# A hybrid transformer step on one core: second part reordered, sixteen z blocks, some elementwise work on GpSimd

## The chip, the cores and the metric

One of the eight cores of a Trainium2 chip runs the whole program in one launch. The metric is the device time of one execution in microseconds (us), a median over executions. The core has a matmul engine (TensorE, PE in the profile; its weight loads are PEld), a vector engine (VectorE, DVE), a scalar engine (ScalarE, ACT), a general one (GpSimd, POOL) and a queue engine that issues most transfers (SyncE, SP).

## The reference

One layer over 512 prompt tokens and 8 x 4 sample tokens, width 2048, everything in float32. In short:

```
xn = rmsnorm(x, g_mix);  proj = xn @ w_in      # q k v iq ik iw xb yb qm
A  = top-k sparse attention (indexer relu scores -> top-k -> softmax over those keys)
B  = RG-LRU(conv4(xb)) * gelu(yb)              # block-diagonal gates, linear recurrence
C  = memory cross-attention(qm, mk, mv)        # 4 heads, 256 memory tokens
x  = x + (sum_n sigmoid(xn @ w_gate[n]) * (branch_n @ w_br[n])) @ w_o
# product-key experts: 16384 experts, 8 heads, 128 x 128 keys, top-16
s  = q(xn2) . sub_keys;  top16 of each half;  top16 of the sums -> expert ids e, weights g
x  = x + sum_k g_k * gelu(u[e_k] . xn2) * v[e_k]
y  = rmsnorm(x, g_final)
```

The outputs are y, the keys and values, the indexer keys, the last convolution inputs, the recurrence's last state and the memory keys and values.

## The kernel before, in words

The 544 tokens are columns and are worked on in two parts: the first (288 columns: 32 sample and 256 prompt tokens, `xF`) and the second (256 prompt columns, `xA`). Every weight goes through one path, a **unit** of 128x1024 numbers (512 KB): `stream` (L233) loads it into a buffer `raw` (L241, SyncE's queue), ScalarE rounds it to `hi` (L221), VectorE makes the rest `lo = raw - hi` (L222), and TensorE does 24 matmuls, for each of 8 chunks hi by x-high, hi by x-low, lo by x-high (L271, L1400). `raw`, `hi` and `lo` are rings of three buffers each (RAW, HL); `widen` adds buffers to the rings for a stage.

The stages in order: memory keys; `branches(0)`, `merge(0)`, `output_proj(0)` for the first part; the first part's expert queries (`pairs(route1, ...)`); `branches(1)`, `merge(1)`, `output_proj(1)` for the second part; the second part's queries, mixed with the first fifty expert rows `up(j)`, and the gate matrices; then sixteen groups, each with the remaining `up(j)`, eight blocks `gated(j)` and `down(g)` (16 units of `v`, then `acc += ...` on VectorE, L1403). `gated(j)` loads a block `gl` (or takes the fresh `ge`), multiplies it by the gate `gt` on VectorE (L1385) and splits it into `zh` (ScalarE) and `zl` (VectorE), rings of nine.

`branches(1)` goes over 45 channels of 128 columns, two units each: first the 8 memory queries (with the memory heads as background work), then the indexer (1 + 8), the 8 queries, keys, values, and last the 16 channels of the recurrence. Attention heads (`attn_head`) and the recurrence (`lru`) start when the selection of the keys is done, beside the last 16 channels; the memory heads' and the indexer's tiles share a pool (`memo`) that closes first.

The side work is written as generators in queues (`Background`): `pump` is called once per chunk (three matmuls), each queue then has rate/8 of a step. bg and bg2 carry heads, selection, attention and recurrence, bg3 the gather: 224 experts' rows of u and 224 of v (1 MB each, fetched by GpSimd's indirect transfers, L1142, and worked on by VectorE with a 128x2048 instruction each, L1190 and L1198) for the first 224 columns. Each row's transfer and its VectorE instruction are tied to the matmul issued last before them (`pace`). Columns 224 and up go through the dense path.

What a scheduler makes of it: instructions are listed per engine by priority (those under `urgent()` first) as far as the scheduler's own model holds them ready; on the chip each engine takes its list strictly in order, and so does SyncE's queue.

Of the kernel before, what the change touches and what calls it, by code (L numbers as in the profile page):

```python
# [35 lines left out]
P0 = NS  # L36
# [5 lines left out]
GL = 4  # L42
AHEAD_UP = 50
# [132 lines left out]
def program(tc, ins, outs):  # L176
# [33 lines left out]
    bg, bg2, bg3 = Background(), Background(), Background()  # L210
    tracks = (bg, bg2, bg3)
# [178 lines left out]
    def branches(part):  # L390
# [5 lines left out]
        prompt = slice(P0 + qbs[0] * 128, P0 + qbs[0] * 128 + HB)  # L396
        pp = None if first else ps_p
        br = ExitStack()
        stg = pool("stage", br)
        ap = pool("ap", br)  # L400
# [61 lines left out]
        mp = pool("mp", memo)  # L462
        if first:
            qms = mp.tile([128, 8, NS], F, name="qms")
            mos = mp.tile([64, 512], F, name="mos")
# [73 lines left out]
        left = bg.queue[-1] if bg.queue else None  # L539
        bg.rate = 1.1 if first else 2.0  # L540
        for h in range(4):
            if h == 3 and not first:
                bg.drain(left)
                route1.weights()
                start_gather()
                rps.close()
                bg3.rate = 0.5
                bg.rate = 1.0
            qm = []
            for i in range(2):  # L550
                s = staged(CH_QM + 2 * h + i)
                if first:
                    nc.vector.tensor_copy(qms[:, 2 * h + i], s[:, :P0])
                qm.append(s)
            bg.add(mem_head(h, qm))
        if first:
            bg.add(mem_sample())


        xp_ = pool("ix", memo)  # L560
# [127 lines left out]
        memo.close()  # L688
# [3 lines left out]
        lp = pool("lr", lrs)  # L692
# [89 lines left out]
        bp = pool("bc", lrs)  # L782

        def attn_head(h):
            n = h // 4
            s = bp.tile([128, HB], F, name="qh", bufs=2)
            nc.sync.dma_start(s, outs["proj"][CH_Q + h, :, prompt])
# [88 lines left out]
        bg.drain()  # L876
        if first:
            nc.sync.dma_start(o_dram[0:8, :, :P0].rearrange("h p s -> p h s"), osm)
        else:
            nc.sync.dma_start(outs["hout"].rearrange("c p n -> p c n"), hl)  # L880
        lrs.close()
# [46 lines left out]
    def output_proj(c0, mo, xg, o0, rs):  # L928
# [5 lines left out]
        for d in range(ND):  # L934
# [8 lines left out]
            add_square(ssum, x2, wp.tile([128, n_], F, name="sq"), d == 0, nc.gpsimd)  # L943
# [13 lines left out]
    rps = ExitStack()  # L957
    rp = pool("rp", rps, side="right")
# [13 lines left out]
    rq = pool("rq", rts)  # L972
    def token_rms(t, c0, rows):
# [35 lines left out]
    class Route:  # L1009
# [14 lines left out]
        def tmp(self, name, dt=F, bufs=2):  # L1024
            return rp.tile([128, 3, 16], dt, name=name, bufs=bufs)[:, :self.nt]

        def lists(self, h, i, qT):

            c = 2 * h + i
            SI = rp.tile([128, 2, 3, 16], F, name=f"si{i}", bufs=LAG)[:, :, :self.nt]  # L1030
# [11 lines left out]
            sc = rp.tile([128, 384], F, name="sc", bufs=3)  # L1042
# [13 lines left out]
        def head(self, h, lists):  # L1056
            nt, ts = self.nt, slice(self.t0, self.t0 + self.nt)
            c2 = rp.tile([128, 2, 3, ncand], F, name="cand", bufs=2)[:, :, :nt]
# [25 lines left out]
        def weights(self):  # L1084
# [5 lines left out]
            sm = rp.tile([128, 24], F, name="gsum")[:, :8 * nt]  # L1090
# [4 lines left out]
    tiles1 = [(0, 128), (128, 128), (256, 32)]  # L1095
    tiles2 = [(0, 128), (128, 128)]
    for t, (c0, rows) in enumerate(tiles1):
        token_rms(t, c0, rows)

    def query(c, xg):  # L1100
        p = project(ins["w_pq"][c], [xg], ND, ps_p)
        qT = rp.tile([128, HA], F, name="qT", bufs=2)[:, :p.shape[-1]]
        with urgent():
            nc.scalar.copy(qT, p)
        return qT

    route1, route2 = Route(0, tiles1), Route(3, tiles2)
    bg2.add(norm())
    bg2.rate = 0.6
    bg.rate = 0.6  # L1110

# [15 lines left out]
    share["pool"] = 0  # L1127
# [345 lines left out]
```

## Time and profile before

| | us |
|---|---|
| median of 3 runs | 4518.69 (4518.44 to 4528.5) |
| profiled execution | 4522.26 |
| its span, first to last instruction | 4520.5 |
| PE busy, share of the span | 4168.4 (92%) |
| DVE busy | 3443.5 (76%) |
| ACT busy | 1930.1 (43%) |
| POOL busy | 1268.6 (28%) |
| mean granted clock of TensorE | 0.961 of full |

A matmul counts as busy for longer than it holds up the next one, so a stretch is read by how many matmuls it issued, not by the busy share. A clock of 1.00 is the upper of TensorE's two levels (2.4 GHz), 0.50 the lower (1.2 GHz). VectorE's average of 76% is made of stages between 48% and 90%.

### The profile page before, as it was taken

The numbers are of one execution on the slowest core, as the hardware profiler recorded it, in microseconds if no ns is written. First come the engines' busy times: TensorE is split into PE (matmuls) and PEld (weight loads), VectorE is DVE, ScalarE is ACT, GpSimd is POOL, SyncE is SP. The second block draws the span as 40 slices with busy tenths as digits, with TensorE's granted clock in tenths as the row PEclk, the third lists the DMA queues.
The fourth block names the chain that finished last, engine by engine and source line by source line (L and its number), as shares of the span: only waits on it lengthen the run. The fifth ranks groups of instructions, "written<-read, shape, count | busy, mean of one in ns | idle before, by whom it ended". The sixth has DMA issues, their size and how long they took to land. (4 is left out here: it accounts for less than half of the span.)

```text
span 4520.5 us, 75499 instructions
## 1 busy us (share of the span) xinstructions
PE 4168.4 (92%) x29283; PEld 3998.3 (88%) x29283; DVE 3443.5 (76%) x5192; ACT 1930.1 (43%) x2940; POOL 1268.6 (28%) x1159
## 2 busy tenths in 40 slices
PE   8999899999986977799889889979999999999998
PEld 7868699999985765799889879979899999999998
DVE  6447444455796875688887899878887999997997
ACT  5334653344432436544443359623333333333333
POOL 3021410001233111345442333312222333322333
PEclk9999999999998987899999999999999999999999
DMA  8656555556546764799987669999988999998995
GB/s 259 216 200 218 162 158 173 166 172 192 174 147 204 271 241 147 254 368 366 364 318 247 225 231 352 371 344 352 341 304 308 371 371 372 368 373 263 380 374 181
DMA packets 381256, 1231.75 MB, mean 272 GB/s; under 512 B 51296, under 2 KB 166752, under 8 KB 319968
## 3 DMA queue, kind: packets, MB, share of 16 engines
q1 hardware_dynamic: 312288, 746.64, 48.6%
q0 software_dynamic: 68608, 480.28, 27.8%
q8 instruction: 230, 3.77, 0.3%
q14 instruction: 130, 1.06, 0.1%
HBM read 1166.46 MB, written 60.22 MB: 271 GB/s over the span
## 5 line engine op out<-in xcount | busy, mean ns | idle before, releaser
L221 ACT CAST hi<-raw 128x1024 fp32r<-128x1024 f32 x1140 | 1191.6, 1049 | 1640.5 <-PE mm L271 821.6
L222 DVE TENSOR_TENSOR lo<-raw,hi 128x1024 fp32r<-128x1024 f32 x1140 | 1424.0, 1253 | 440.2 <-ACT hi L221 430.2
L271 PE MATMUL mm<-xgd,hi 128*128 128x320 f32 (+1 forms) x4608 | 1011.7, 309 | 4.0 <-ACT hi L221 4.0
L271 PEld LDWEIGHTS mm<-xgd,hi 128*128 128x128 f32 x4608 | 766.1, 189 | 4.3 <-ACT hi L221 4.2
L271 PE MATMUL mm<-xgd,lo 128*128 128x320 f32 (+1 forms) x2304 | 711.6, 309 | 21.1 <-DVE lo L222 21.0
L1400 PE MATMUL mm<-zh,hi 128*128 128x320 f32 x2048 | 638.8, 313 | 44.4 <-ACT zh L221 40.2
L1400 PE MATMUL mm<-zh,lo 128*128 128x320 f32 x2048 | 638.2, 313 | 9.8 <-DVE lo L222 9.6
L1142 POOL DMA_INDIRECT row<-in_un,idx x224 | 380.7, 1699 | 927.6 <-PE mm L271 388.9
L1400 PE MATMUL mm<-zl,hi 128*128 128x320 f32 x2048 | 638.1, 312 | 1.6 <-DVE zl L222 1.6
L271 PE MATMUL mm<-xF,hi 128*128 128x288 f32 x2976 | 624.2, 303 | 2.1 <-ACT stage L424 1.4
L1142 POOL DMA_INDIRECT row<-in_vn,idx x224 | 406.0, 1813 | 756.3 <-PE mm L1400 242.3
L271 PE MATMUL mm<-xA,hi 128*128 128x256 f32 x2976 | 550.7, 287 | 27.9 <-ACT hi L221 18.4
L1198 DVE SCALAR_TENSOR_TENSOR gacc<-row,hv,gacc 128x2048 f32<-128x2048 f32 x221 | 521.8, 2361 | 52.5 <-DMA row<-in_vn,idx 30.7
L1190 DVE SCALAR_TENSOR_TENSOR row<-row,xnat 128x2048 f32<-128x2048 f32 x224 | 513.3, 2292 | 55.6 <-DMA row<-in_un,idx 18.4
L271 PEld LDWEIGHTS mm<-xA,hi 128*128 128x128 f32 x2976 | 467.7, 193 | 42.2 <-ACT hi L221 20.3
L271 PEld LDWEIGHTS mm<-xF,hi 128*128 128x128 f32 x2976 | 483.7, 189 | 23.1 <-issue 17.6
L271 PEld LDWEIGHTS mm<-xgd,lo 128*128 128x128 f32 x2304 | 435.6, 189 | 27.3 <-DVE lo L222 27.0
L271 PE MATMUL mm<-xF,lo 128*128 128x288 f32 x1488 | 445.7, 300 | 0.0
L271 PE MATMUL mm<-xA,lo 128*128 128x256 f32 x1488 | 426.7, 287 | 10.4 <-DVE lo L222 10.3
L1400 PEld LDWEIGHTS mm<-zh,hi 128*128 128x128 f32 x2048 | 390.3, 191 | 48.4 <-ACT zh L221 42.5
L1400 PEld LDWEIGHTS mm<-zh,lo 128*128 128x128 f32 x2048 | 390.2, 191 | 12.5 <-DVE lo L222 12.3
L1400 PEld LDWEIGHTS mm<-zl,hi 128*128 128x128 f32 x2048 | 390.1, 191 | 3.3 <-DVE zl L222 2.9
(370 smaller groups left out, 6317.8 us busy)
## 6 DMA issues: line engine op xcount, KB each, us to landing
raw<-in_u SPq DMA_DIRECT2D x256, 512.0 KB, 7.1
raw<-in_v SPq DMA_DIRECT2D x256, 512.0 KB, 7.0
raw<-in_w_gate SPq DMA_DIRECT2D x192, 512.0 KB, 4.9
raw<-in_w_in SPq DMA_DIRECT2D x180, 512.0 KB, 4.4
raw<-in_w_br SPq DMA_DIRECT2D x96, 512.0 KB, 3.7
raw<-in_w_pq SPq DMA_DIRECT2D x64, 512.0 KB, 4.4
raw<-in_w_o SPq DMA_DIRECT2D x64, 512.0 KB, 4.6
g_dram<-gs SPq DMA_DIRECT2D x10, 2048.0 KB, 7.6
```

Of the source, the lines that this page charges most:

```text
L221: nc.scalar.copy(hi, src)
L222: eng.tensor_tensor(lo, src, hi.bitcast(F), op=OP.subtract)
L271: last["mm"] = nc.tensor.matmul(p[:, i, :n], a[:, s], chunk(b[which], u + k), start=(u + k == 0 and pr == 0), stop=(u + k == k_chunks - 1 ...
L1142: i = nc.gpsimd.indirect_dma_start(out=r, out_offset=None, in_=ins[table], in_offset=bass.IndirectOffsetOnAxis(ap=ind[:, s:s + 1], axis=0))
L1190: j = nc.vector.scalar_tensor_tensor(r, r, 1.0, xn, op0=OP.mult, op1=OP.mult, accum_out=h)
L1198: j = nc.vector.scalar_tensor_tensor(acc, r, h, acc, op0=OP.mult, op1=OP.add)
L1400: last["mm"] = nc.tensor.matmul(p[:, 0, :NTA], a[:, s], b, start=(k == 0 and pr == 0), stop=(k == 7 and pr == 2))
```

## The change

Seven things change.

1. `branches(1)`: the memory queries and heads move behind keys and values, before the recurrence's channels. The first 8 channels are now the indexer's. `start_gather` moves from behind six memory channels to behind the fourth indexer channel. The recurrence gets a queue of its own (bg4), the heads' next query is loaded one head ahead (`load_q`), and the rates change (attention 1.1 instead of 1.6).
2. The first part's third token tile (32 columns of a 288-column part) is taken out of `route1`: its query columns are kept in `qk`, and `odd_lists` makes its lists and heads beside the second part's indexer.
3. While `share["pool"]` is 4 (first part's queries, all of `branches(1)`, second part's queries up to three `up` behind them) the low part of every fourth unit is made by GpSimd instead of VectorE: 8 of 32 units, 23 of 90, and 18 of the queries and rows behind.
4. `gated`: the product of block and gate goes to GpSimd, 128 times.
5. The rings `zh` and `zl` grow from nine to sixteen; for that `widen(zs0, 2, 0)` goes, so in the last stage the ring `raw` has three buffers instead of five.
6. The last four additions of squares in `output_proj` go from GpSimd to VectorE.
7. The gather's rate: 0.53 instead of 0.5 in `merge(1)`, 0.85 instead of 0.7 beside the gate matrices, 0.52 instead of 0.68 in the first seven groups of the last stage, 0.72 instead of 0.7 after. The gate matrices start two `up` later.

```
+ZB = 16
...
-        left = bg.queue[-1] if bg.queue else None
-        bg.rate = 1.1 if first else 2.0
-        for h in range(4):
-            if h == 3 and not first:
-                bg.drain(left)
-                route1.weights()
-                start_gather()
-                rps.close()
-                bg3.rate = 0.5
-                bg.rate = 1.0
-            qm = []
...
+        def mem_channels():
+            for h in range(4):
+                qm = []
+                for i in range(2):
+                    s = staged(CH_QM + 2 * h + i)
...
+                bg.add(mem_head(h, qm))
+
         if first:
+            open_memory()
+            bg.rate = 1.1
+            mem_channels()
             bg.add(mem_sample())
+        else:
+            left = bg.queue[-1]
+            bg.add(odd_lists())
+            bg.rate = 2.4
...
             bg2.add(dots(c, s))
+            if c == 3 and not first:
+                bg.drain(left)
+                route1.weights()
+                start_gather()
+                bg3.rate = 0.5
+                bg.rate = 1.7
...
+        def load_q(h):
+            qh[h] = bp.tile([128, HB], F, name="qh", bufs=2)
+            nc.sync.dma_start(qh[h], outs["proj"][CH_Q + h, :, prompt])
...
-        bg.rate = 2.5
-        bg2.rate = 2.2 if first else 1.6
+        bg4.rate = 2.2
+        bg2.rate = 2.2 if first else 1.1
+        if not first:
+            memo = ExitStack()
+            open_memory()
+            bg.rate = 0.8
+            mem_channels()
         for c in range(8):
             xb = staged(CH_XB + c)
             yb = staged(CH_YB + c)
-            bg.add(lru(c, xb, yb))
+            bg4.add(lru(c, xb, yb))
...
-            add_square(ssum, x2, wp.tile([128, n_], F, name="sq"), d == 0, nc.gpsimd)
+            add_square(ssum, x2, wp.tile([128, n_], F, name="sq"), d == 0, nc.vector if d >= 12 else nc.gpsimd)
...
+    def odd_lists():
+        route, ls = Route(2, [(0, NS)]), []
+        for c in range(16):
+            ls.append(route.lists(*divmod(c, 2), qk[:, c]))
+            yield
+            if c % 2:
+                yield from route.head(c // 2, ls[-2:])
+                yield
+        route.weights()
...
-    share["pool"] = 0
+    share["pool"] = 4
     wide = ExitStack()
     widen(wide, 1, 0)
-    pairs(route1, lambda c: query(c, xgF), lambda c: None)
+    pairs(route1, lambda c: query(c, xgF, 0), lambda c: None)
...
     route2.weights()
-    up(next(ups))
+    for _ in range(3):
+        up(next(ups))
     rps.close()
+    share["pool"] = 0
...
-    bg3.rate = 0.7
+    bg3.rate = 0.85
...
-    widen(zs0, 2, 0)
...
-        zh = zp.tile([128, NTA], R, name="zh", bufs=9)
-        zl = zp.tile([128, NTA], R, name="zl", bufs=9)
+        zh = zp.tile([128, NTA], R, name="zh", bufs=ZB)
+        zl = zp.tile([128, NTA], R, name="zl", bufs=ZB)
...
-        nc.vector.tensor_tensor(ev_, ev_, zt["g"][:, :, j % 4], op=OP.mult)
+        nc.gpsimd.tensor_tensor(ev_, ev_, zt["g"][:, :, j % 4], op=OP.mult)
...
-        bg3.rate = 0.68 if 8 * g < AHEAD_UP else 0.7
+        bg3.rate = 0.52 if 8 * g < AHEAD_UP else 0.72
```

TensorE's list at the end of the second part's channels, before: `mm<-xA` are units (the last ones here belong to the first gates of `merge(1)`), `kT,qh` an attention head's scores, `cst,ex` its transposes, `pT,vN` its products, `xc,w_rg` and `xc,w_ig` a recurrence channel's gates.

```order
L802 MATMUL w_17855<-cst,ex 128x128 x3
L792 MATMUL w_17881<-kT,qh 128x512
L802 MATMUL w_17907<-cst,ex 128x128 x4
L809 MATMUL w_17949<-pT,vN 128x256 x3
L809 MATMUL w_17949<-pT,vN 128x128
L745 MATMUL w_17968<-xc,w_rg 128x256
L745 MATMUL w_17989<-xc,w_ig 128x256
L745 MATMUL w_18138<-xc,w_rg 128x256
L745 MATMUL w_18159<-xc,w_ig 128x256
L745 MATMUL w_18288<-xc,w_rg 128x256
L745 MATMUL w_18294<-xc,w_ig 128x256
L271 MATMUL mm<-xA_86,hi 128x256
```

The same place in the change:

```order
L272 MATMUL mm<-xA_86,lo 128x256
L764 MATMUL w_18282<-xc,w_rg 128x256
L764 MATMUL w_18303<-xc,w_ig 128x256
L764 MATMUL w_18449<-xc,w_rg 128x256
L764 MATMUL w_18470<-xc,w_ig 128x256
L764 MATMUL w_18599<-xc,w_rg 128x256
L764 MATMUL w_18605<-xc,w_ig 128x256
L272 MATMUL mm<-xA_86,hi 128x256
```

Before, 22 rows of side work (of which the last eleven stand here) lie between two units, among them the last three attention heads; now six rows of the last three recurrence channels.

VectorE's list around the end of the first group of the last stage, before: `acc` ends an output block of `down`, `gl<-gl,gt` is the product with the gate, `zl` the low part of a z block, `lo` that of a unit, `gacc` and `row` are gathered rows.

```order
L222 TENSOR_TENSOR zl<-gl,zh 128x320
L1198 SCALAR_TENSOR_TENSOR gacc<-row,hv_14746,gacc 128x2048
L1403 TENSOR_TENSOR acc<-mm,acc 128x320
L222 TENSOR_TENSOR lo<-raw,hi 128x1024
L222 TENSOR_TENSOR zl<-gl,zh 128x320 x3
L1385 TENSOR_TENSOR gl<-gl,gt 128x320
L222 TENSOR_TENSOR zl<-gl,zh 128x320
L1385 TENSOR_TENSOR gl<-gl,gt 128x320 x2
L1190 SCALAR_TENSOR_TENSOR row,hv_14746<-row,xnat 128x2048
L222 TENSOR_TENSOR zl<-gl,zh 128x320 x2
L1385 TENSOR_TENSOR gl<-gl,gt 128x320 x2
L1403 TENSOR_TENSOR acc<-mm,acc 128x320
```

In the change, in the middle of the first group:

```order
L223 TENSOR_TENSOR lo<-raw,hi 128x1024
L1451 TENSOR_TENSOR acc<-mm,acc 128x320
L223 TENSOR_TENSOR lo<-raw,hi 128x1024
L223 TENSOR_TENSOR zl<-gl,zh 128x320 x2
L1244 SCALAR_TENSOR_TENSOR gacc<-row,hv_14607,gacc 128x2048
L1451 TENSOR_TENSOR acc<-mm,acc 128x320
L223 TENSOR_TENSOR lo<-raw,hi 128x1024
L223 TENSOR_TENSOR zl<-gl,zh 128x320
L1451 TENSOR_TENSOR acc<-mm,acc 128x320
L223 TENSOR_TENSOR zl<-gl,zh 128x320 x2
```

The z blocks' low parts, before in a bunch with the products where one group ends, now lie singly between output blocks of the group before.

GpSimd's list in the same stage of the change, where before there were only gathered rows (`row<-in_un`, `row<-in_vn`):

```order
L1433 TENSOR_TENSOR gl<-gl,gt 128x320 x4
L1188 DMA row<-in_un,idx_14458 128x2048 x2
L1433 TENSOR_TENSOR gl<-gl,gt 128x320 x4
L1188 DMA row<-in_un,idx_14458 128x2048
L1433 TENSOR_TENSOR gl<-gl,gt 128x320 x4
L1188 DMA row<-in_vn,idx_14458 128x2048
L1433 TENSOR_TENSOR gl<-gl,gt 128x320 x4
```

The products stand in front of rows that the program writes before them, and rows stand behind products that wait for a block's load.

## Rows read from the trace of the kernel before

**Rows 1.** Windows by stage; columns as the first line names them, count in brackets.

```profile
core 0: us, PE busy (x) PEld busy (x) DVE busy (x) ACT busy (x) POOL busy (x), PEclk, DMA share, GB/s
1167.00:1308.00 141.00, 127.96 (x895) 121.24 (x893) 127.22 (x501) 52.83 (x112) 44.89 (x110) 0.94 0.48 146
1308.00:1500.00 192.00, 144.25 (x973) 125.94 (x972) 148.27 (x349) 69.19 (x122) 61.74 (x75) 0.89 0.56 182
1500.00:1648.00 148.00, 140.62 (x1107) 133.69 (x1107) 134.04 (x177) 54.97 (x72) 31.27 (x24) 0.99 0.87 315
1648.00:1842.00 194.00, 106.03 (x502) 82.18 (x501) 101.55 (x224) 118.81 (x169) 29.57 (x37) 0.69 0.39 131
1842.00:2260.00 418.00, 402.84 (x3384) 401.87 (x3384) 363.15 (x336) 182.72 (x236) 193.62 (x103) 0.99 0.95 361
2379.00:2668.00 289.00, 248.99 (x1787) 244.00 (x1787) 244.67 (x587) 95.42 (x135) 97.95 (x167) 0.95 0.66 224
2668.00:2968.00 300.00, 284.36 (x2071) 282.69 (x2070) 267.62 (x409) 224.40 (x512) 88.42 (x42) 0.97 0.92 348
2968.00:3350.00 382.00, 347.97 (x2227) 340.99 (x2228) 326.62 (x375) 116.68 (x145) 102.66 (x63) 0.95 0.94 346
3450.00:4500.00 1050.00, 1044.84 (x7121) 1041.72 (x7120) 932.91 (x1025) 385.63 (x500) 339.56 (x230) 1.00 0.93 346
```

**Rows 2.** TensorE's groups, 1308 to 1843: busy us, mean ns | idle before and releasers.

```profile
L802 PE MATMUL w<-cst,ex 128*128 128x128 f32 x56 | 13.8, 385 | 33.7 <-DVE ex L455 33.6
...
L483 PE MATMUL w<-cst,mex 128*128 128x128 f32 x16 | 3.8, 326 | 37.6 <-DVE mex L455 37.4
```

**Rows 3.** TensorE's timeline, 1770 to 1843: start us, us, instruction, idle before it.

```profile
1770.25 0.40 PE L271 MATMUL mm<-xA,lo 128*128 128x256 f32 x1
...
1805.32 1.06 PE L745 MATMUL w<-xc,w_rg 128*128 128x256 f32 x2
...
1841.79 0.80 PE L271 MATMUL mm<-xA,hi 128*128 128x256 f32 x2 [17.07 <-ACT hi L221]
```

**Rows 4.** VectorE's groups by form, whole span.

```profile
L222 DVE TENSOR_TENSOR lo<-raw,hi 128x1024 fp32r<-128x1024 f32 x1140 | 1424.0, 1253 | 440.2 <-ACT hi L221 430.2 <-PE w L615 4.8 <-PE mm L271 2.3
...
L1198 DVE SCALAR_TENSOR_TENSOR gacc<-row,hv,gacc 128x2048 f32<-128x2048 f32 x221 | 521.8, 2361 | 52.5 <-DMA row<-in_vn,idx 30.7 <-PE mm L271 15.6 <-PE mm L1400 5.7
...
L1385 DVE TENSOR_TENSOR ge<-ge,gt 128x320 f32<-128x320 f32 x78 | 37.9, 486 | 0.4 <-ACT ge L1268 0.4
```

**Rows 5.** GpSimd's groups by form, whole span.

```profile
L920 POOL TENSOR_TENSOR m<-m,sg 128x256 f32<-128x256 f32 x32 | 48.1, 1505 | 82.0 <-DVE sg L919 74.1 <-DVE hv L1194 4.1 <-issue 3.8
L920 POOL TENSOR_TENSOR m<-m,sg 128x288 f32<-128x288 f32 x32 | 25.8, 807 | 418.3 <-DVE sg L919 418.3
```

**Rows 6.** Timeline of VectorE and GpSimd, 2003 to 2012.

```profile
2007.27 2.88 DVE L222 TENSOR_TENSOR lo<-raw,hi 128x1024 fp32r<-128x1024 f32 x2
...
2007.49 1.58 POOL L920 TENSOR_TENSOR m<-m,sg 128x256 f32<-128x256 f32 x1 [1.93 <-DVE sg L919]
```

**Rows 7.** TensorE's groups, 2379 to 2668.

```profile
L271 PE MATMUL mm<-xgd,lo 128*128 128x320 f32 (+1 forms) x573 | 174.0, 304 | 17.2 <-DVE lo L222 17.2
...
L1289 PE MATMUL w<-cst,f 128*128 128x128 f32 x1 | 0.4, 447 | 17.5 <-DVE f L1281 17.5
```

**Rows 8.** TensorE's groups, 2968 to 3350.

```profile
L1400 PE MATMUL mm<-zh,hi 128*128 128x320 f32 x743 | 234.8, 320 | 44.4 <-ACT zh L221 40.2 <-DVE acc L1403 2.9 <-ACT hi L221 1.4
```

**Rows 9.** TensorE's timeline from 2967.

```profile
2968.25 0.64 PE L1400 MATMUL mm<-zh,hi 128*128 128x320 f32 x1 [15.87 <-ACT zh L221]
```

**Rows 10.** Transfers issued 3500 to 4050: count, KB each, median us to landing.

```profile
raw<-in_v SPq DMA_DIRECT2D x80, 512.0 KB, 6.8
raw<-in_u SPq DMA_DIRECT2D x76, 512.0 KB, 8.2
```

**Rows 11.** ScalarE's groups by form, whole span.

```profile
L221 ACT CAST hi<-raw 128x1024 fp32r<-128x1024 f32 x1140 | 1191.6, 1049 | 1640.5 <-PE mm L271 821.6 <-PE mm L1400 536.4 <-DMA raw<-in_w_in 82.2
```

**Rows 12.** Transfers issued 1500 to 1640.

```profile
raw<-in_w_in SPq DMA_DIRECT2D x42, 512.0 KB, 5.4
```

More of the change, by code (lines that the diff above doesn't have):

```diff
@@ L209, in program @@
     g_dram = dr.tile([NTA // 32, 128, 128, 32], F, name="g_dram")
-    bg, bg2, bg3 = Background(), Background(), Background()
-    tracks = (bg, bg2, bg3)
+    bg, bg2, bg3, bg4 = (Background() for _ in range(4))
+    tracks = (bg, bg2, bg4, bg3)
     def pump():
@@ L396, in branches @@
         prompt = slice(P0 + qbs[0] * 128, P0 + qbs[0] * 128 + HB)
+        side = "left" if first else "right"
         pp = None if first else ps_p
         br = ExitStack()
-        stg = pool("stage", br)
-        ap = pool("ap", br)
+        stg = pool("stage", br, side=side)
+        ap = pool("ap", br, side=side)
         bias = {qb: ap.tile([128, (qb + 1) * 128], F, name=f"bias{qb}") if qb else caus for qb in qbs}
@@ L461, in branches, with open_memory @@
         memo = ExitStack()
[L462 to L465, printed above, removed]
+        mp = None
+        def open_memory():
+            nonlocal mp, qms, mos
+            mp = pool("mp", memo, side=side)
+            if first:
+                qms = mp.tile([128, 8, NS], F, name="qms")
+                mos = mp.tile([64, 512], F, name="mos")
+        qms = mos = None
         def mem_head(h, qm):
@@ L687, in branches @@
         bg2.drain()
-        memo.close()
+        ixs.close()
+        if first:
+            memo.close()
+        else:
+            rps.close()
         lrs = ExitStack()
-        lp = pool("lr", lrs)
+        lp = pool("lr", lrs, side=side)
         if first:
@@ L779, in lru @@
             yield
-        bp = pool("bc", lrs)
+        bp = pool("bc", lrs, side=side)
+        qh = {}
+        def load_q(h):
+            qh[h] = bp.tile([128, HB], F, name="qh", bufs=2)
+            nc.sync.dma_start(qh[h], outs["proj"][CH_Q + h, :, prompt])
         def attn_head(h):
             n = h // 4
-            s = bp.tile([128, HB], F, name="qh", bufs=2)
-            nc.sync.dma_start(s, outs["proj"][CH_Q + h, :, prompt])
+            if h == 0:
+                load_q(0)
+            if h < 7:
+                load_q(h + 1)
+            s = qh.pop(h)
             pT = bp.tile([128, qbs[-1] + 1, HB], F, name="pT")
@@ L1093, in weights, with query @@
             nc.vector.tensor_tensor(g, g, sm[:, :, None].to_broadcast([128, 8 * nt, 16]), op=OP.mult)
-    tiles1 = [(0, 128), (128, 128), (256, 32)]
-    tiles2 = [(0, 128), (128, 128)]
-    for t, (c0, rows) in enumerate(tiles1):
+    tiles = [(0, 128), (128, 128)]
+    qk = rq.tile([128, 16, NS], F, name="qk")
+    for t, (c0, rows) in enumerate(tiles + [(256, NS)]):
         token_rms(t, c0, rows)
-    def query(c, xg):
+    def query(c, xg, c0):
         p = project(ins["w_pq"][c], [xg], ND, ps_p)
@@ L1237, in program @@
     map_ = pool("ma", mas)
-    bg3.rate = 0.5
+    bg3.rate = 0.53
     widen(wide, 2, 2, "right")
@@ L1335, in gate_matrix @@
             nc.sync.dma_start(g_dram[g0 + i], gs)
-    for t, (c0, rows) in enumerate(tiles2):
+    for t, (c0, rows) in enumerate(tiles):
         token_rms(3 + t, HA + c0, rows)
@@ L1341, in program @@
     bg3.rate = 0.3
-    share["pool"] = 0
-    pairs(route2, lambda c: query(c, xg2), up)
+    share["pool"] = 4
+    pairs(route2, lambda c: query(c, xg2, HA), up)
     ups = iter(range(16, AHEAD_UP))
@@ L1347, in program @@
     route2.weights()
-    up(next(ups))
+    for _ in range(3):
+        up(next(ups))
     rps.close()
+    share["pool"] = 0
     ras = ExitStack()
```

33 lines of the change are left out of this document (17 added, 16 removed).

## The prediction

> **What bounds the kernel now.** I read the windows by stage first, then TensorE's groups and timeline where a stage loses time, then the other engines' groups by form, and last the transfers from issue to landing.
>
> The windows give the pace. With 256 columns 3384 matmuls take 418 us, 0.1235 us each; with 320 columns 7121 take 1050 us, 0.1474 us each [rows 1]. In both the granted clock is at the upper level (0.99, 1.00) and TensorE issues without gaps, so there a change can only lose. A stage loses what its time exceeds its count of matmuls times this pace. Part two up to the end of its channels (1167 to 1842, four windows [rows 1]) issues 895 + 973 + 1107 + 502 = 3477 matmuls, about 429 us of 675. The second part's queries (2379 to 2668) need 1787 x 0.1474 = 263 of 289. The first groups of the last stage (2968 to 3350) need 2227 x 0.1474 = 328 of 382 [rows 1].
>
> What part two waits for is mostly VectorE and the order that TensorE must keep: 33.6 us for the softmaxes of the attention heads and 37.4 for those of the memory heads, both on VectorE [rows 2]. VectorE is busy for 127.22 + 148.27 + 134.04 + 101.55 = 511 of the 675 us, 76%; it reaches 91% (134.04 of 148) only from 1500 to 1648, where gathered rows fill it [rows 1]. At the end the last unit's matmul stands at 1770.25 and the next at 1841.79, with side work alone between them and the clock at 0.69 over that window [rows 1, 3].
>
> **Part two: low parts to GpSimd, new order.** The change takes 31 low parts off VectorE here: 31 x 1.253 = 39 us [rows 4]. GpSimd's price for a 128x1024 product of two inputs has no row. By its 128x288 row, 0.807 us with nothing beside it, it is 0.807 x 1024/288 = 2.87 us; by the 128x256 row, 1.505 us among VectorE's gather work, 6.0 us [rows 5]. I take 2.9. Both engines slow each other: two low parts on VectorE took 2.88 us instead of 2 x 1.253 = 2.51 while a GpSimd instruction of 1.58 us ran, 0.23 us for each us of it [rows 4, 6]. So VectorE pays 31 x 2.9 x 0.23 = 20 us back, and its work is 511 - 39 + 20 = 492 us. Three low parts may exist at a time, so a late one holds up TensorE only when the two units ahead of it are used up, 2 x 24 x 0.1235 = 5.9 us: 2.9 is hidden, 6.0 just isn't.
>
> The Trainium skill, "GPSIMD Engine Reference", section "4.1 Engine selection", sends elementwise add and multiply on a tile to VectorE, since GpSimd is about half as fast with two inputs (4497 against 2293 ns). By that ratio, an estimate, the low part would take 1.96 x 1.253 = 2.5 us, and 3 us would be paid back less. The rows agree in direction (2.9 against 1.25). The rule speaks against this part; rival D is what it would be if it decided.
>
> The order matters more. The tail of 71.5 us without a unit (1770.25 to 1841.79) holds, after the change, only the gates of the last three recurrence channels instead of also three attention heads. Before, these channels start at 1805.32 and the next unit runs at 1841.79, so 36.5 us stay [rows 3]. The memory heads, with their waits of 37.4 us [rows 2], go behind keys and values, where units and attention heads run beside them; on SyncE their loads and stores go past those of 12 channels, and each attention head's query is asked for one head earlier, so neither stands in front of a unit that needs it. With nothing left to wait on but VectorE, I let it run at the share of its best window, 134.04/148 = 0.906 [rows 1]. The tail keeps VectorE at that window's 101.55/194 = 0.52, so 19 us of its 492 lie in the tail: (492 - 19)/0.906 + 36.5 = 559 us, a gain of 116. If its share stayed at 0.76, 492/0.757 = 650 and the gain is 25, less some 7 for rows that are gathered earlier, 18; if VectorE never idled the gain is 183. I choose a little above the middle, since two named waits of 71 us and 35 us of tail are what goes, 106 together.
>
> **Second part's queries.** 18 low parts move: 18 x (1.253 - 0.66) = 11 us of VectorE time. TensorE waits 17.2 us for low parts there, and 17.5 us for the row `f` that the gate matrices need [rows 7]; two more `up` (2 x 48 x 0.1474 = 14 us) now stand ahead of these. Between 0 and 35 us I take 20. Four additions of squares go to VectorE in `output_proj`; at no more than a product's 0.486 us [rows 4] that is 2 us, counted 0.
>
> **Gate matrices.** The gather's rate goes from 0.7 to 0.85, about 8 rows of 2.36 us [rows 4], 19 us more for VectorE in a window where it has 300 - 267.62 = 32 idle [rows 1]. Bounds 0 and 19, taken 5.
>
> **Last stage, z blocks.** The loss of 54 us in its first groups is at most 40.2 us of waiting for `zh` [rows 8]: nine blocks let ScalarE split only the first block of the next group early. 15.87 us of that is the first block of all [rows 9], which no ring helps. Sixteen blocks remove the rest and the stalls behind it: 54 less 16 leaves 38 as the most, 0 the least; I take 33. The 128 products take 128 x 0.486 = 62 us off VectorE [rows 4]; on GpSimd, by the two rows of before, one takes 0.90 to 1.88 us [rows 5], 128 of them 115 to 241, which gives VectorE 26 to 55 us back. VectorE isn't what the last stage waits for (932.91 of 1050, [rows 1]): counted 0. Behind a product that waits for its block, gathered rows queue on GpSimd; VectorE's gather instructions come later, not TensorE.
>
> **Last stage, the ring of raw weights, five to three.** A buffer is loaded again when its low part is done, and its own high part can't start before the unit three back has left TensorE. So in three units' time, 72 x 0.1474 = 10.6 us, must fit the landing (6.8 us for v, 8.2 for u [rows 10]), then the high part (1.049 us [rows 11]) and the low part (1.253 [rows 4]): 9.1 and 10.5 us. The ratio to 10.6 is 0.86 and 0.99, before any wait in VectorE's queue, where a 2.36 us gather instruction [rows 4] often stands ahead. The nearest row of three buffers beside gathered rows is the window from 1500 to 1648: landing 5.4 us [rows 12], 7.7 of 72 x 0.1235 = 8.9, ratio 0.87, and it took 148 us for 1107 x 0.1235 = 137, that is 0.24 us over for each of 46 units. The last stage has 256 units of v and 152 of u left, 408: 98 us at that price. That window has other waits too, so 0 is the lower bound; above, the 152 units at 0.99 may pay half a gather instruction per turn of three, (2.36/2)/3 = 0.39 us, 60 us more, 158. I take 70, 0.17 us per unit.
>
> **Sum.** 4522.3 (the profiled execution) - 116 - 20 + 5 - 33 + 70 = 4428. That execution is 3.6 above the median of 4518.69, so 4425.
>
> **Rivals.**
>
> B, the ring of three costs nothing: six us of finished units ahead absorb late landings and the slower gather (0.52 for 0.68) thins the traffic. For it: medians of 9.1 and 10.5 lie under 10.6. Against it: they are medians, with transfers at 0.93 of the engines' time [rows 1], and a late one makes the next late. 4425 - 70 = 4355.
>
> C, the ring decides the last stage, and the kernel is slower. Place: each load of `in_v` and `in_u` from 2968 on. If each low part also waits for one gather instruction, a turn is 7.5 + 2.3 + 2.36 = 12.2 us for three units, 4.05 us instead of 3.54: 0.52 x 408 = 212. 4425 - 70 + 212 = 4567. It decides from 164 us, 0.40 us per unit. For it: the u units' 10.5 us leave 0.1 for any wait, and VectorE is busy 89% of the time there (932.91 of 1050 [rows 1]); against it: those 62 us of products go.
>
> D, part two gains 18 us only: low parts on GpSimd come late, as the 1.505 us row [rows 5] would have it, or its side work keeps VectorE from its units as now. 4425 + 98 = 4523, no change. For it: four chains of softmax remain on VectorE; against it: the named waits. The rule of the Trainium skill cited above, weighed as a result of its own, is this one.
>
> **How the numbers follow.** My forecast 0.42, B 0.27, C 0.14, D 0.17. About 0.3% (14 us) is what a measurement can tell from no change. The forecast's own range, a part-two gain of 80 to 150 about its 116, is 4390 to 4460 and B's 4320 to 4390. D splits into no change (0.08), faster (0.05) and slower (0.04); C is slower; one in a hundred of the forecast is no change. Faster 0.73, same 0.09, slower 0.18. From 4340 to 4550 lie the forecast, most of B, D, and the lower third of C.
>
> **What would show it.** In the changed profile: from the first part's queries to the first gate unit 559 us instead of 675, with the gap between units at its end near 36; GpSimd's low parts at 2.9 us, VectorE's beside them longer than 1.253. TensorE's wait for `zh` near 16 instead of 40. In the last stage the pace per 24 matmuls 3.7 us instead of 3.54, with idle time released by `hi` and, behind that, by loads of `raw`. If the pace stays at 3.54 it is B; at 3.94 or more C; if part two still takes over 640 us, D.

## The result and the profile after

The change is slower: 4569.69 us (median of 4 executions) against 4518.56, ratio 1.0096 on record, 95% interval 1.0072 to 1.0121 (the two medians alone give 1.0113). The forecast was 4425. Rival C's number, 4567, came out, but by other costs than C's.

The profiled execution's span is 4566.1 us against 4520.5. Windows of the change and of before, cut at the same instructions of TensorE (first unit of the first part's queries, first gate unit after the hole, first unit of `output_proj(1)`, first block of the last stage, end), columns as in [rows 1]. The change:

```profile
1162.97:1813.22 650.25, 520.10 (x3472) 460.56 (x3470) 506.00 (x1251) 293.58 (x468) 295.77 (x432) 0.90 0.60 199
1813.22:2241.48 428.26, 406.50 (x3385) 405.35 (x3385) 371.27 (x348) 186.89 (x243) 173.53 (x107) 0.97 0.95 364
2966.22:4566.00 1599.78, 1506.97 (x9992) 1480.63 (x9992) 1309.29 (x1369) 543.90 (x706) 590.38 (x432) 0.98 0.87 318
```

Before:

```profile
1166.98:1841.79 674.81, 518.66 (x3471) 462.86 (x3469) 510.87 (x1248) 295.76 (x471) 167.48 (x245) 0.87 0.56 189
1841.79:2260.65 418.86, 403.05 (x3385) 402.08 (x3385) 363.38 (x337) 183.36 (x236) 193.62 (x103) 0.98 0.95 361
2968.25:4520.00 1551.75, 1489.74 (x9992) 1478.21 (x9992) 1338.04 (x1514) 543.45 (x707) 461.68 (x318) 0.98 0.91 336
```

The stretch up to the end of part two's channels, called part two from here on, gained 24.6 us, where 116 were forecast. The merge behind them lost 9.4, with 371.27 us of VectorE's work instead of 363.38, and `output_proj(1)` 3.0. The queries, rows and gate matrices between it and the last stage lost 14.1 (605.2 to 619.3). The last stage lost 48.0. The start was 4.0 shorter.

**Part two.** A hole is a stretch in which TensorE runs no unit. The change has two long ones. The one in the middle:

```profile
1569.66 0.28 PE L272 MATMUL mm<-xA,lo 128*128 128x256 f32 x1
1593.52 1.08 PE L830 MATMUL w<-cst,ex 128*128 128x128 f32 x4 [23.58 <-DVE ex L457]
...
1604.99 0.82 PE L272 MATMUL mm<-xA,hi 128*128 128x256 f32 x2
```

The one at the end:

```profile
1763.96 0.28 PE L272 MATMUL mm<-xA,lo 128*128 128x256 f32 x1
...
1813.22 0.79 PE L272 MATMUL mm<-xA,hi 128*128 128x256 f32 x2 [18.75 <-ACT hi L222]
```

The tail of [rows 3] shrank from 71.5 to 49.3 us, not to 36.5. ScalarE is busy for 36.3 us of these 49.3, of them 21.8 in 17 loads of function tables (1.28 us each). The memory heads' waits of [rows 2] are nearly gone (37.4 to 4.1 us). The attention heads' are not (33.6 to 31.7): the first head's softmax holds units up for 35.3 us (1569.66 to 1604.99). It stands in TensorE's list between units while VectorE is busy until 1590 with the selection of the keys and with four gathered rows (10.8 us) among its steps. Before, the same place had a hole of 40.8 us, which began with 14.5 us of waiting for a head's query:

```profile
1648.28 0.28 PE L271 MATMUL mm<-xA,lo 128*128 128x256 f32 x1
...
1689.03 0.78 PE L271 MATMUL mm<-xA,hi 128*128 128x256 f32 x2
```

Between the holes TensorE waits more for units' low parts, 37.3 us instead of 9.5. The change (us in total, times, longest):

```profile
PE mm L272 <- DVE lo L223: 27.5, 22, 2.7
PE mm L272 <- POOL lo L223: 9.8, 4, 3.8
```

Before:

```profile
PE mm L271 <- DVE lo L222: 9.5, 10, 2.4
```

VectorE, which makes most of them, waits more for the lists' steps on GpSimd. Its waits over the stretch, the change:

```profile
DVE t L1053 <- POOL cand L1097: 29.2, 12, 5.3
DVE ev L1116 <- POOL eq L1111: 7.3, 7, 1.7
DVE ev L1113 <- POOL eq L1111: 6.6, 4, 1.7
...
DVE t L1053 <- POOL j L1069: 4.4, 2, 2.5
```

Before:

```profile
DVE ev L1078 <- POOL eq L1076: 4.5, 4, 1.6
DVE ev L1081 <- POOL eq L1076: 3.7, 4, 1.7
DVE t L1018 <- POOL cand L1062: 3.5, 2, 3.1
```

That is 47.5 us against 11.7.

**Last stage.** TensorE waits there less for `zh` (26.6 us, of it 22.19 the first block's, [rows 8, 9]) and more for low parts. VectorE's waits say what these wait for; the change:

```profile
DVE lo L223 <- ACT hi L222: 155.6, 138, 11.0
DVE zl L223 <- ACT zh L222: 57.6, 47, 10.6
```

Before:

```profile
DVE lo L222 <- ACT hi L221: 27.5, 58, 2.4
```

High parts are late because their `raw` is. ScalarE's waits for the loads of `v`, the change and before:

```profile
ACT hi L222 <- DMA raw<-in_v: 342.4, 131, 13.4
```

```profile
ACT hi L221 <- DMA raw<-in_v: 6.9, 3, 3.7
```

The landings themselves hardly changed ([rows 10]: 6.8 and 8.2); transfers of the change issued 3500 to 4050:

```profile
raw<-in_v SPq DMA_DIRECT2D x78, 512.0 KB, 7.5
raw<-in_u SPq DMA_DIRECT2D x68, 512.0 KB, 7.6
```

GpSimd's new work, whole span, and VectorE's low parts in the last stage (1217 ns before):

```profile
L223 POOL TENSOR_TENSOR lo<-raw,hi 128x1024 fp32r<-128x1024 f32 x49 | 122.7, 2503 | 101.6 <-ACT hi L222 85.0 <-DVE rsN L1011 16.3
L1433 POOL TENSOR_TENSOR ge<-ge,gt 128x320 f32<-128x320 f32 x78 | 120.4, 1544 | 256.9 <-ACT ge L1315 219.7 <-DVE ge L1314 29.9 <-issue 7.0
...
L1433 POOL TENSOR_TENSOR gl<-gl,gt 128x320 f32<-128x320 f32 x50 | 62.0, 1268 | 65.1 <-DMA gl<-ge_dram 50.5 <-issue 11.9 <-DVE zl L223 1.8
```

```profile
L223 DVE TENSOR_TENSOR lo<-raw,hi 128x1024 fp32r<-128x1024 f32 x409 | 518.1, 1268 | 156.7 <-ACT hi L222 155.6
```

### The profile page after: what moved, and what is told of

It reads as the page before. It is cut to its first block, busy times and chain, and to the rows that moved or that the text cites. A ratio compares the mean times of both kernels' runs of the same rounds, so it can differ in the third digit from the quotient of the medians.

```text
span 4566.1 us, 75861 instructions
## 1 busy us (share of the span) xinstructions
PE 4204.4 (92%) x29283; PEld 4009.6 (88%) x29283; DVE 3431.5 (75%) x5058; ACT 1934.9 (42%) x2945; POOL 1506.3 (33%) x1472
## 5 line engine op out<-in xcount | busy, mean ns | idle before, releaser
L223 DVE TENSOR_TENSOR lo<-raw,hi 128x1024 fp32r<-128x1024 f32 x1091 | 1388.8, 1277 | 522.4 <-ACT hi L222 514.7
L272 PE MATMUL mm<-xgd,hi 128*128 128x320 f32 (+1 forms) x4608 | 1027.3, 312 | 5.3 <-ACT hi L222 5.0
L272 PEld LDWEIGHTS mm<-xgd,hi 128*128 128x128 f32 x4608 | 777.8, 191 | 6.6 <-ACT hi L222 6.5
L272 PE MATMUL mm<-xgd,lo 128*128 128x320 f32 (+1 forms) x2304 | 721.9, 313 | 47.0 <-DVE lo L223 41.9
L1448 PE MATMUL mm<-zh,hi 128*128 128x320 f32 x2048 | 639.7, 313 | 40.5 <-ACT zh L222 26.6
L272 PE MATMUL mm<-xA,hi 128*128 128x256 f32 x2976 | 562.1, 290 | 18.7 <-ACT hi L222 18.7
L1244 DVE SCALAR_TENSOR_TENSOR gacc<-row,hv,gacc 128x2048 f32<-128x2048 f32 x221 | 537.9, 2434 | 36.6 <-PE mm L272 16.3
L1236 DVE SCALAR_TENSOR_TENSOR row<-row,xnat 128x2048 f32<-128x2048 f32 x224 | 539.0, 2406 | 30.2 <-DMA row<-in_un,idx 15.9
L1188 POOL DMA_INDIRECT row<-in_un,idx x224 | 334.4, 1493 | 679.6 <-PE mm L272 203.2
L1188 POOL DMA_INDIRECT row<-in_vn,idx x224 | 352.1, 1572 | 557.2 <-PE mm L272 144.4
L272 PE MATMUL mm<-xA,lo 128*128 128x256 f32 x1488 | 432.5, 291 | 31.5 <-DVE lo L223 23.9
```

The source lines that it names most:

```text
L223: eng.tensor_tensor(lo, src, hi.bitcast(F), op=OP.subtract)
L272: last["mm"] = nc.tensor.matmul(p[:, i, :n], a[:, s], chunk(b[which], u + k), start=(u + k == 0 and pr == 0), stop=(u + k == k_chunks - 1 ...
L1188: i = nc.gpsimd.indirect_dma_start(out=r, out_offset=None, in_=ins[table], in_offset=bass.IndirectOffsetOnAxis(ap=ind[:, s:s + 1], axis=0))
L1236: j = nc.vector.scalar_tensor_tensor(r, r, 1.0, xn, op0=OP.mult, op1=OP.mult, accum_out=h)
L1244: j = nc.vector.scalar_tensor_tensor(acc, r, h, acc, op0=OP.mult, op1=OP.add)
L1448: last["mm"] = nc.tensor.matmul(p[:, 0, :NTA], a[:, s], b, start=(k == 0 and pr == 0), stop=(k == 7 and pr == 2))
```

## The experiments

The runs came from several chips on which the kernel before took 4519 to 4553 us; most of that difference lies in the first part's channels (476 to 514 us), which no experiment touches. So each has its ratio to the kernel before on its own chip, and the stages are compared by windows of one profile each. Kernels with the same last stage differ there by up to 9 us (1502.5 in `c_bestv`, 1511.6 in `d_lru`), so a smaller difference of two profiles shows little by itself. "Last stage" and "part two" are the windows above.

**First four: ring, products, low parts, each alone.** `a_ring5` is the change with

```
-ZB = 16
+ZB = 13
...
+    widen(zs0, 2, 0)
```

> The change with the ring of raw weights back at five buffers in the last stage; the z blocks' rings are thirteen instead of sixteen to make room. Theory 1 (the ring of three is what costs the last stage): the eight late groups of 768 matmuls fall from about 120 to 113 us each and the whole is 50 to 70 us shorter, 4500 to 4520. Theory 2 (the last stage is longer because of the products on GpSimd or the later gather): the groups stay at 118 to 120 us, the whole within 10 us of the change's 4570.

Ratio 0.9982 (0.9966 to 0.9998).

`b_ring3` is the kernel before with

```
-    widen(zs0, 2, 0)
```

> The kernel before with one line less: the ring of raw weights has three buffers in the last stage instead of five, all else as before. Theory 1 (the ring of three alone costs the last stage): 60 to 90 us longer, 4580 to 4605, each late group at 120 us instead of 112.6. Theory 2 (ring and products or gather together): under 30 us.

Ratio 1.0094 (1.0065 to 1.0123).

`a_zvec` is the change with

```
-        nc.gpsimd.tensor_tensor(ev_, ev_, zt["g"][:, :, j % 4], op=OP.mult)
+        nc.vector.tensor_tensor(ev_, ev_, zt["g"][:, :, j % 4], op=OP.mult)
```

> The change with the 128 products of z block and gate on VectorE again. Theory 1 (only the ring counts in the last stage): within 10 us of the change's 4570. Theory 2 (products on GpSimd wait behind gathered rows, delay blocks and slow VectorE): 15 to 40 us shorter, with the waits for the z blocks' high parts below the change's 26.6 us.

Ratio 1.0014 (0.9999 to 1.0028).

Last stages of the three, in this order:

```profile
2997.80:4541.00 1543.20, 1485.52 (x9992) 1474.16 (x9992) 1307.89 (x1369) 541.01 (x706) 636.31 (x432) 0.98 0.89 329
```

```profile
2991.00:4582.00 1591.00, 1511.73 (x9992) 1485.69 (x9992) 1335.58 (x1514) 541.06 (x707) 398.89 (x318) 0.98 0.90 328
```

```profile
2994.20:4552.00 1557.80, 1501.70 (x9992) 1476.33 (x9992) 1306.10 (x1495) 541.88 (x706) 376.83 (x305) 0.98 0.89 327
```

Five buffers, with thirteen z blocks instead of sixteen, give back 57 us of the change's 1599.8; three cost the kernel before 39, which lies between the two ranges. Theory 1 holds for the ring in the change, and in the kernel before about half of it. But the products on GpSimd cost 42 us as well, theory 2's size: two causes, not one. With five buffers VectorE's wait for `hi` falls from 155.6 to 39.9 us:

```profile
DVE lo L223 <- ACT hi L222: 39.9, 65, 5.0
```

`a_pool0` is the change with

```
-    share["pool"] = 4
+    share["pool"] = 0
     wide = ExitStack()
```

> The change with all low parts on VectorE from the first part's queries to the end of the second part's channels (the queries of the second part keep theirs on GpSimd). Theory 3 (low parts on GpSimd stand ahead of the lists' steps on GpSimd that VectorE waits for): VectorE's waits for GpSimd between 1163 and 1560 fall from 48 us to 15 or less, and part two to the end of its channels is 15 to 35 us shorter. Theory 4 (the low parts relieve VectorE by 39 us as forecast, and the order is what fails): that stretch is 10 to 40 us longer.

Ratio 1.0073 (1.0047 to 1.0099). Part two:

```profile
1193.74:1834.13 640.39, 514.32 (x3472) 451.88 (x3470) 510.29 (x1281) 293.62 (x466) 219.80 (x401) 0.90 0.61 202
```

It is 9.9 us shorter than in the change, so theory 4 falls. Other profiles agree: part two takes 650.2 to 652.3 us in the three with this order and low parts on GpSimd, 638.0 to 643.6 in the seven with all of them on VectorE. Theory 3 gets the sign only: the waits for the lists' steps stay at 40.4 us (`cand` 23.9), so they belong to the new order, not to the low parts. What the row shows is that 31 low parts, 39 us, raise VectorE's work by 4.3 us only (506.00 to 510.29) when they come back: beside GpSimd's work VectorE's other instructions had taken nearly as much longer. The same 39 gathered rows, for one, took 99.4 us in the change and 88.8 here.

**Next four: the costs together, and what bounds part two.** `c_best` is the change with `a_pool0`'s and `a_ring5`'s lines and

```
-    share["pool"] = 4
+    share["pool"] = 0
     pairs(route2, lambda c: query(c, xg2, HA), up)
```

and `c_bestv` also has `a_zvec`'s line.

> The change with all low parts on VectorE everywhere and the ring of raw weights at five buffers in the last stage (z rings of thirteen); order, products on GpSimd and rates stay. If the two costs found add up (56 us by the ring, 20 by the low parts in part two), it is 70 to 85 us shorter than the change, that is 25 to 45 us shorter than the kernel before on the same chip. In the stage of the second part's queries, 605 us before and 619 in the change: 605 to 612 if the low parts on GpSimd lengthened it, 617 to 622 if the gather's rate or the order did.

Ratio 0.9935 (0.9921 to 0.9949): 29 us shorter than the kernel before, as expected.

> As the run before it, with the products on VectorE as well. With five buffers VectorE's queue is not on the path, so the products' engine should matter by less than 10 us either way in the last stage (1544 with five buffers and products on GpSimd). The rival, that products on GpSimd slow VectorE and the blocks whatever the ring, expects 15 us or more in favour of VectorE: 1530 or less.

Ratio 0.9844 (0.9828 to 0.986), 4454.55 against 4523.09 us: faster than both kernels. The last stages:

```profile
2956.80:4504.00 1547.20, 1488.96 (x9992) 1477.84 (x9992) 1307.96 (x1369) 541.46 (x706) 637.35 (x432) 0.98 0.89 328
```

```profile
2954.50:4457.00 1502.50, 1472.38 (x9992) 1466.27 (x9992) 1308.42 (x1495) 542.54 (x706) 433.94 (x305) 0.99 0.91 338
```

My expectation for `c_bestv` fell: with five buffers the products still cost 44.7 us. The four last stages make a table in which both costs nearly add:

| last stage, us | products on VectorE | products on GpSimd |
|---|---|---|
| five raw buffers, 13 z blocks | 1502.5 | 1543.2 and 1547.2 |
| three raw buffers, 16 z blocks | 1557.8 | 1599.8 |

And VectorE's work is the same in both columns, 1308.42 and 1307.96: taking 62 us of products off it relieved it by nothing. `c_best`'s stage of the second part's queries and gates took 618.7 us, `c_bestv`'s 612.2, so its loss isn't the low parts alone.

`c_bpool4` is the kernel before with GpSimd's low parts from the first part's queries to the end of `branches(1)`:

```
-    share["pool"] = 0
+    share["pool"] = 4
     wide = ExitStack()
...
     wide.close()
-    share["pool"] = 0
...
     branches(1)
+    share["pool"] = 0
```

> The kernel before with every fourth low part made by GpSimd from the first part's queries to the end of the second part's channels, nothing else. Theory 3 (low parts on GpSimd delay the lists' steps there, and VectorE waits): the stretch from the first query to the first gate unit, 675 us before, becomes 5 to 25 us longer. Theory 4 (39 us are taken off an engine that part two waits for): 15 to 40 us shorter.

Ratio 1.0003 (0.9992 to 1.0015). Part two is 5.2 us longer, at theory 3's edge; VectorE's work falls by 9.1 us (510.87 to 501.77), not 39:

```profile
1157.76:1837.78 680.02, 523.67 (x3471) 467.75 (x3470) 501.77 (x1218) 299.14 (x474) 245.44 (x276) 0.89 0.56 188
```

`c_nogath` is `a_pool0` with

```
                 start_gather()
-                bg3.rate = 0.5
+                bg3.rate = 0.0
```

> The change with all low parts of part two on VectorE and with the gathered rows' rate at zero until the second part's channels are done (they are made later, so only part two counts here). It takes about 70 instructions of 2.4 us, 165 us, off VectorE in part two. Theory 5 (part two is bound by VectorE's work, as the forecast had it): the stretch from the first query to the first gate unit falls from 640 us by 100 or more. Theory 6 (it is bound by the chain selection, softmax, recurrence in TensorE's fixed order): it falls by less than 50, and the hole without a unit at its end stays at 45 to 50.

```profile
1162.24:1728.90 566.66, 502.53 (x3472) 446.60 (x3470) 427.05 (x1215) 285.02 (x459) 133.59 (x361) 0.96 0.50 154
```

The first gate unit in it, behind the hole at the end:

```profile
1728.87 0.79 PE L272 MATMUL mm<-xA,hi 128*128 128x256 f32 x2 [21.52 <-ACT hi L222]
```

Between the theories: VectorE's work fell by 83.2 us (to 427.05; the 165 I had expected counted too many rows, there are 39) and the stretch by 73.7, 0.89 us per us. VectorE's share is 0.75, though, so its sum isn't the bound. The gain lies in the two holes. The middle one, 54.7 us in `a_pool0`, is gone (no gap between units there is over 5 us), and the one at the end falls from 50.3 to 21.8 us; TensorE's waits for low parts stay as they were (21.8 and 21.9). In `a_pool0` ten gathered rows, 22.2 us, stand in VectorE's list inside the middle hole, among the selection's steps that the first softmax waits for. Without rows the gates of all recurrence channels run before the last unit. (Done later, the rows lengthen the last stage; one execution took 4588.69 us.)

**Then the mechanism of the products, the z ring, and two attempts at more.** `d_zlpool` is `c_best` with

```
-        split(zh, zl, e)
+        split(zh, zl, e, nc.gpsimd)
```

> The change with all low parts of units on VectorE and five raw buffers in the last stage, products on GpSimd as in the change, and the z blocks' low parts on GpSimd too. Theory 7 (VectorE stands on a z block's low part, which waits for the high part of a product that is late in GpSimd's queue, and the units' low parts are queued behind it): VectorE has no such wait left (53 us before), and the last stage falls from 1548 to 1505 to 1525 us though GpSimd works 190 us more. Theory 8 (GpSimd's work slows VectorE's instructions): the last stage stays at 1540 to 1565.

Ratio 1.0016 (1.0001 to 1.0032). Both ranges missed: the last stage is 33 us longer than `c_best`'s, though VectorE no longer waits for `zh`. The run doesn't decide against theory 7, since it adds costs of its own. Another 62 us of work left VectorE's list and again none came off its busy time (1309.60), VectorE's low parts take 1356 ns, and VectorE waits for gathered rows, which GpSimd now starts late (40.5 us against 24.4 in `c_best` and 12.3 in `c_bestv`):

```profile
2961.90:4542.00 1580.10, 1493.72 (x9992) 1477.02 (x9992) 1309.60 (x1241) 539.66 (x706) 840.95 (x560) 0.98 0.88 321
```

```profile
L223 DVE TENSOR_TENSOR lo<-raw,hi 128x1024 fp32r<-128x1024 f32 x409 | 553.6, 1356 | 57.1 <-ACT hi L222 52.8 <-DMA raw<-in_v 4.0
```

```profile
DVE gacc L1244 <- DMA row<-in_vn,idx: 40.5, 31, 6.5
```

`b_z13` is the kernel before with

```
-        zh = zp.tile([128, NTA], R, name="zh", bufs=9)
-        zl = zp.tile([128, NTA], R, name="zl", bufs=9)
+        zh = zp.tile([128, NTA], R, name="zh", bufs=13)
+        zl = zp.tile([128, NTA], R, name="zl", bufs=13)
```

> The kernel before with rings of thirteen z blocks instead of nine, nothing else (five raw buffers, products on VectorE). The forecast's term: the first groups of the last stage lose 33 us less, the whole is 25 to 40 us shorter, the last stage 1512 to 1527 us instead of 1552. Rival: the gather's slower rate in the first groups gave most of what the last stage gained (1503 with everything on VectorE and five buffers): under 15 us shorter.

Ratio 0.996 (0.9943 to 0.9977), 18 us shorter as a whole, between the two ranges. The last stage is 9 us shorter than the 1551.75 of before, and 17 shorter than in `c_bpool4`, which has the same last stage as the kernel before and took 1560.0 there; neither is 33. The rival is nearer.

```profile
2983.20:4526.00 1542.80, 1484.29 (x9992) 1475.61 (x9992) 1337.47 (x1514) 545.38 (x707) 451.25 (x318) 0.98 0.91 338
```

`d_lru` is `c_bestv` with the first of these edits, `d_gath` with the second:

```
-        bg4.rate = 2.2
+        bg4.rate = 3.4
```

```
                 start_gather()
-                bg3.rate = 0.5
+                bg3.rate = 0.25
```

> The change with all low parts and products on VectorE and five raw buffers in the last stage, and the recurrence's rate 3.4 instead of 2.2. If the hole of 50 us without a unit at the end of part two is recurrence work that the program takes up too late, the hole falls by 15 us or more and so does the whole. If it is the chain of the last channels (each starts only after its own projection), hole and time stay within 8 us.

Ratio 0.9843 (0.9827 to 0.9859). The hole stays at 50.5 us: the rate isn't the cause. The expectation's other branch, the chain of the last channels, doesn't follow from it, since in `c_nogath` that chain leaves a hole of 21.8 us only.

> The same kernel with the recurrence's rate as it was and the gathered rows' rate 0.25 instead of 0.5 in part two. Without any rows part two was 74 us shorter for about 165 us of VectorE work, 0.45 us per us; half of them less should give 30 to 40 us there. These rows come later, where VectorE is busy for 87 to 94%: the whole is 10 to 25 us shorter if they find room in the gate matrices and the first groups, or equal to 40 us longer if the last rows come after TensorE's end.

Ratio 0.989 (0.9872 to 0.9908), slower than `c_bestv`. Part two gained 28 us on `c_bestv`'s 638.0, and the last stage lost 43. The gain is again the middle hole, 19.8 us instead of 55.6 and now without a gathered row in it; the one at the end stays at 48.7.

```profile
1182.04:1791.89 609.85, 512.16 (x3471) 453.39 (x3469) 467.71 (x1252) 293.98 (x466) 183.98 (x381) 0.92 0.56 178
```

**Last two: GpSimd's work without anyone waiting for it.** `e_two` is `c_bestv` with, behind each block's split,

```
+        nc.gpsimd.tensor_tensor(dm.rearrange("p (g t) -> p g t", t=32), zh.bitcast(F).rearrange("p (g t) -> p g t", t=32),
+                                zt["g"][:, :, j % 4], op=OP.mult)
```

and `e_one` with

```
+        for _ in range(2):
+            nc.gpsimd.tensor_copy(dm, zh.bitcast(F))
```

> The change with all low parts and products on VectorE and five raw buffers in the last stage (1503 us in that stage), and on GpSimd 128 more products of two inputs of the size of the moved ones (high part of the block by the gate), whose result nobody reads. If what costs is that blocks wait for the product, the last stage stays within 8 us. If what costs is GpSimd's work itself (it slows VectorE's instructions or delays the gathered rows in its own queue), the last stage is 20 to 45 us longer, as with the products moved (1545).

> The same with two copies (one input each) of the block's high part on GpSimd in place of each extra product, again read by nobody. If instructions with two inputs slow VectorE and copies don't, VectorE's 128x1024 low parts stay at 1.22 us and the last stage within 10 us of 1503. If time in GpSimd's queue is what counts, the last stage is as much longer as with the extra products, per us of GpSimd's work.

Ratios 0.9916 (0.9895 to 0.9936) and 0.988 (0.986 to 0.9901). The last stage of `e_two`, its low parts and the added work:

```profile
2967.30:4513.00 1545.70, 1489.38 (x9992) 1476.95 (x9992) 1374.87 (x1495) 541.73 (x706) 652.82 (x433) 0.98 0.90 329
```

```profile
L223 DVE TENSOR_TENSOR lo<-raw,hi 128x1024 fp32r<-128x1024 f32 x409 | 529.7, 1296 | 28.6 <-ACT hi L222 28.2
```

```profile
L1437 POOL TENSOR_TENSOR dm<-zh,gt 128x320 f32<-128x320 f32 x128 | 215.9, 1687 | 203.5 <-ACT zh L222 143.9 <-issue 25.6 <-DVE ge L1435 25.1
```

The same of `e_one`, without the low parts:

```profile
2978.50:4494.00 1515.50, 1476.96 (x9992) 1465.98 (x9992) 1350.96 (x1495) 542.96 (x706) 735.92 (x561) 0.99 0.91 335
```

```profile
L1438 POOL COPY dm<-zh 128x320 f32<-128x320 f32 x256 | 297.6, 1163 | 148.2 <-ACT zh L222 125.8 <-issue 13.1
```

215.9 us of products that nobody reads make VectorE's own work 66.5 us longer (1308.42 to 1374.87), 0.31 us for each us, and the last stage 43.2 us (33 by the ratios). 297.6 us of copies give 42.5 us, 0.14 for each, and 13.0 us of time (16 by the ratios; just outside the expected 10), though they hold GpSimd's queue for longer; VectorE's low parts took 1251 ns beside them, so copies slow VectorE too. So two-input work on GpSimd, beside an unchanged list of VectorE's, costs about what the moved products cost, and time in GpSimd's queue is a small part of it.

The moved products are not quite that case. They leave VectorE's work as long as it was (1308.42 in `c_bestv`, 1307.96 in `c_best`), so the slowing explains why nothing was gained. The 44.7 us themselves are time in which VectorE stands still: at `zl` 53.0 us, where `c_bestv` has 3,

```profile
DVE zl L223 <- ACT zh L222: 53.0, 46, 7.5
```

and TensorE's waits for units' low parts grow from 7.5 to 29.3 us. This is read from the traces; no run has the slowing without the late products, or the reverse.

## Why the prediction was wrong

- **Part two, "I let it run at the share of its best window": the step that failed.** VectorE's work came out near, 506 us against 492. Its share did not rise to 0.906; it is 506.00/650.25 = 0.78. "With nothing left to wait on but VectorE" was not so. Of the two named waits (71 us) the memory heads' went, but the attention heads' stayed (31.7 us of 33.6), the tail kept 49.3 us instead of 36.5, and TensorE's waits for low parts grew from 9.5 to 37.3 us, beside 36 us more in which VectorE waits for the lists' steps on GpSimd. I counted what the old order loses and not what the new one does. 91.4 us of the 145 by which I was wrong lie here. The lower bound of the same paragraph, an unchanged share of 0.76, gave 650 us, and 650.3 were measured; that it fits so closely is luck, as work and share were both a little higher. The best window was also misread: 0.9 is reached not only beside gathered rows. From 1167 to 1308 it is 127.22/141 = 0.90 without one, and 112.60/141 = 0.80 in the change. And rows don't just fill gaps: `c_nogath` and `d_gath` show them ahead of the steps that the first softmax waits for.
- **Low parts to GpSimd.** The price of one, 2.9 us, was close (2.50), though the row of 0.807 us that it came from did not have "nothing beside it": a low part on VectorE ran during 56% of it. The payback was not: 20 us were expected back of 39, but VectorE's work fell by 4.3 us only (4 to 9 by the three profiles with this order), and by 9.1 in the old order. The 0.23 us per us came from one pair of instructions; the runs give 0.31 in the last stage.
- **Products "counted 0".** They cost 41 to 45 us. The payback range (26 to 55 us) was too small, since all 62 us were given back. That VectorE isn't what the last stage waits for fell too: 66 us more work in `e_two` cost 43 us, and where VectorE stood at late `zl` in `c_best`, TensorE waited behind it. On the slowing, the Trainium skill, "GPSIMD Engine Reference", section "8. Key points", says that GpSimd shares its interfaces to the on-chip memory with VectorE and contends there with VectorE's instructions of two inputs from it or in a two-port mode. The trace agrees for the low part, which has two: 1217 to 1268 ns.
- **Ring of three, +70.** Right in mechanism and size: 57 us in the change (0.14 us per unit instead of 0.17), 39 in the kernel before, 55 with products on VectorE. The sign of it is VectorE waiting for `hi`, 27.5 to 155.6 us.
- **z blocks, -33.** Thirteen alone give 9 to 17 by the profiles and 18 by the ratio. The waits for `zh` went as forecast, except that the first block's grew from 15.87 to 22.19, but low parts `zl` and units' low parts were late next. That the last stage's sum came near (37 us longer forecast, 48.0 measured) is luck: products cost 42 us where 0 was counted, and without ring and products the stage is 49 us shorter (1551.75 to 1502.5 in `c_bestv`) where 33 were counted. The rest of the gain in `c_bestv`'s last stage (1502.5) needs the gather's slower rate or the fewer rows left; this wasn't tried apart.
- **Queries and gates, -20 and +5.** +14.1 instead. With low parts on GpSimd the stage took 619.3 to 624.1 us in five kernels, with all of them on VectorE 606.0 to 618.7 in seven, and 601.1 to 605.2 in four with the old order and rate. So the low parts lengthened it too; what of the change did the rest stays open, as does the merge's 9.4 us.
- **Rivals.** D was right in its price (18 of 24.6 us) and in the half of its reason that VectorE stays away from units; late low parts were a small part (9.8 us of TensorE's waits). C had the total by accident: its ring cost 212, and 57 were measured.

## What to carry to other kernels

Work moved from VectorE to GpSimd is priced by what VectorE's busy time falls by, not by what leaves its list: here 62 us moved and 0 were relieved, 39 moved and 4 to 9 were relieved. When an order is changed, price the stretch by the engine share that it has now, and ask of each wait that goes which chain is next and what else stands in the engine's list ahead of it. In part two that was gathered rows ahead of the first softmax, which a share of busy time doesn't show. A shorter ring is measured by the sum of landing and the steps that free a buffer against the time of its turns; at 0.86 and 0.99 it cost 39 to 57 us here.

## What was not expected of the hardware

- Copies on GpSimd, with one input, slow VectorE too: 0.14 us per us against 0.31 for products. A copy of 128x320 took 1.163 us, nearly a product's price (1.268 and 1.544).
- The first part's channels took 480.1 and 482.8 us in the profiles of before and the change, 508.8 to 514.3 in those of `a_ring5`, `a_zvec`, `a_pool0` and `b_ring3`, and 476.0 to 484.3 in the next four, with nearly the same instructions there: more than most edits here move. It goes with the group of runs and not with the kernel (`b_ring3` has the old order). The granted clock there was 0.97 in the change and 0.94 in `a_pool0`; why stays open.
